# Reordering attention's SBUF pools and moving the w_down block sums into attention

## The chip, the cores and the metric

The kernel runs on one core of a Trainium2 chip. Its engines are TensorE (PE: matmuls, with PEld for its weight loads), VectorE (DVE), ScalarE (ACT), GpSimd (POOL) and SyncE (SP, which here only issues DMAs, one after the other, from one queue). The metric is the time of one execution on the device in microseconds (us).

## The reference

One layer of a bidirectional encoder over two sequences (2048 and 256 tokens of width 1024), in float32:

```python
h = rms_norm(x)
q_lat, kv_lat, z, xbc, dt = split(h @ w_in)
mla = rms_norm(softmax_attention(q_lat, kv_lat))   # 8 heads, dense over all positions
ssd = ssd_mixer(z, xbc, dt)                        # conv, forward and backward chunked scans, gate, norm
x = x + concat(mla, ssd) @ w_out
h = rms_norm(x)
y = rms_norm(x + (silu(h @ w_gate) * (h @ w_up)) @ w_down)
```

## The kernel before

Tokens are cut into 18 tiles of 128 (16 of the first sequence, 2 of the second). Every large matmul is done as three (`mm3`): both operands are split into a high part and a rest, by a copy on ACT or POOL and a subtraction on DVE (`split_w`, `split_ps`, `split`).

The stages, in order of time: (a) the input projection, whose queries, keys and values go to DRAM; (b) conv and forward scan, with the projection weights `wx0` to `wx7`, and small tables (`rows`, `offs`) loaded for each chunk by `load_rows` for `decays`; (c) attention, 8 heads of 5 query blocks (four of four tiles against 2048 keys, one of two tiles against 256); (d) `gather` (backward scan, gate, norms), `turned` (transposes) and `project` (w_out); (e) gate and up projections, in three parts of six tiles, each of 11 steps j, done as seven products of 2x2 blocks in Strassen's manner (`group`, `weights`); (f) the down projection, also of seven products, with the left operands read back from DRAM (`operand`) and the right ones (`columns`) either w_down's blocks or differences of two of them. These differences, the block sums `d_B`, are made by `sums(j)` in the last part of stage e: two loads of 512 KB into tiles `o`, four subtractions on POOL and four stores.

SBUF is handed out as stacks. The left stack after `decays` holds in stage b: `b_w0` (8 KB per partition, `wx0`), `b_st` (8), `b_w` (24), `b_w2` (32: `wx4` to `wx7`), `b_m` (12.5: `rows`, `offs`, `to`), `b_sb` (76: conv and scan tiles). In stage c the 36 KB of `mla` come first, then `c_l` (28: `pT`, `ot`), `c_q` (8), `c_kv0` (27: keys and values of even heads), `c_sb` (about 46: scores), `c_kv1` (odd heads). So the first keys lie at 72 to 99 KB, over `b_m` and the start of `b_sb`, and the first queries at 64 to 72, over `b_w2`. In stage d after `mla`: `d_st` (8: raw w_out), `d_sb` (28: `y2`, `z2`, `sc`, `ct`), `d_w` (68: split w_out, `grow`), `d_m` (24). The four tiles `o` (`op`, 4 KB each) stand on the right, from the end of stage b on, and are not used in attention. A new tile waits only for the tiles whose bytes it takes (`reuse_waits="tile"`).

The order of each queue is fixed at compile time: by a planner that walks the program with a model of time, except that inside `tc.manual_schedule(engines=...)` the named engines keep the order of the program. That holds in attention from its second block on for PE, ACT and DVE. SP's order, and the first block's, are the planner's.

Of the kernel before, what the change touches and what calls it, by code (L numbers as in the profile page):

```python
# [11 lines left out]
F32 = mybir.dt.float32  # L12
F32R = mybir.dt.float32r
I32 = mybir.dt.int32
AF = mybir.ActivationFunctionType
ALU = mybir.AluOpType
# [4 lines left out]
P = 128  # L21
D = 1024
KD = D // P
# [9 lines left out]
NF = FF // P  # L33
# [8 lines left out]
def hymba_kernel(ctx: ExitStack, tc: tile.TileContext, io, seqs, dbg=None):  # L42

    nc = tc.nc
# [26 lines left out]
    dram = ctx.enter_context(tc.tile_pool(name="dram", bufs=1, space=DRAM))  # L71
# [39 lines left out]
    def pool(stack, name, bufs, **kw):  # L111
        return stack.enter_context(tc.tile_pool(name=name, bufs=bufs, reuse_waits="tile", **kw))
# [6 lines left out]
    def split_w(hi, lo, raw, eng="pool"):  # L119
        if eng == "pool":  # L120
            nc.gpsimd.tensor_scalar(hi, raw, 1.0, 0.0, op0=ALU.mult, op1=ALU.add)
        elif eng == "act":
            nc.scalar.activation(hi, raw, AF.Copy)  # L123
        else:
            nc.vector.tensor_copy(hi, raw)
        nc.vector.tensor_tensor(lo, raw, f(hi), op=ALU.subtract)  # L126
# [248 lines left out]
    with ExitStack() as ph:  # L375
        wp0 = pool(ph, "b_w0", 1)
        st = pool(ph, "b_st", 2)
# [3 lines left out]
        with ExitStack() as inner:  # L381
            sb = pool(inner, "t_sb", 1)

            def tmp(name):
                return sb.tile([P, NT, 16], F32, name=name)
# [7 lines left out]
            u, e, s, s2, w = (tmp(f"sp{i}") for i in range(5))  # L393
# [27 lines left out]
        mp = pool(ph, "b_m", 1)  # L421
# [14 lines left out]
        for j in range(KD):  # L436
            raw = st.tile([P, KD, P], F32, name="rawx", tag="rawx")
# [56 lines left out]
        for d in range(2):  # L494
            r = mp.tile([P, SH, P], F32R, name=f"rows{d}")
            o = mp.tile([P, P], F32R, name=f"offs{d}")
            raw = sb.tile([P, SH + 1, P], F32, name="rk", tag="Y")
# [130 lines left out]
        for b in range(nb + 2):  # L628
            parts = {}
# [30 lines left out]
    op = pool(ctx, "e_o", 4, side="right")  # L660
# [5 lines left out]
        mla[t0, nt] = t  # L666


    with ExitStack() as ph:
        lp = pool(ph, "c_l", 2)  # L670
        qp = pool(ph, "c_q", 2)
        kvs = [pool(ph, "c_kv0", 1)]
        sb = pool(ph, "c_sb", 2)
        kvs.append(pool(ph, "c_kv1", 1))

# [5 lines left out]
        def step(hold=False):  # L681
            more = bool(turn)
            if turn:
                held.append(turn.popleft()())
                if not hold:
                    release()
            while len(prod) > LAG or (prod and not more):
                prod.popleft()()
                if not more:
                    break  # L690
            if late and late[0][0] <= count[0]:
                late.popleft()[1]()
            count[0] += 1
# [5 lines left out]
        def load_head(h):  # L699
            kv = kvs[h % 2]  # L700
            k = kv.tile([QKD, 2, T], F32R, name="k", tag="k")
            nc.sync.dma_start(f(k)[:NOPE], d_k[h // 2][(h % 2) * NOPE:(h % 2 + 1) * NOPE])
            nc.sync.dma_start(f(k)[NOPE:], d_kr)
            v = kv.tile([P, NT, P], F32R, name="v", tag="v")
            nc.sync.dma_start(f(v), d_v[:, h, :].rearrange("(t p) d -> p t d", p=P))
            return k, v

        def block(h, k, v, t0, nt, s0, sn):
# [93 lines left out]
            for kt in range(sn):  # L802
                turn.append(lambda kt=kt: turned(kt))
# [4 lines left out]
        def next_block():  # L808
            h, *rest = work.pop(0)
            if h not in heads:  # L810
                heads[h] = load_head(h)
            block(h, *heads[h], *rest)

        next_block()
        with tc.manual_schedule(engines={mybir.EngineType.PE, mybir.EngineType.Activation, mybir.EngineType.DVE}):
            while work:
                next_block()
            while tail:
                tail.popleft()()
            while turn or prod or late:  # L820
                step()
# [7 lines left out]
    parts = [(order[i:i + G], order[i + G:i + 2 * G]) for i in range(0, NT, 2 * G)]  # L829
# [11 lines left out]
        H[s, half] = h  # L841

    with ExitStack() as ph:
        st = pool(ph, "d_st", 2)
        sb = pool(ph, "d_sb", 2)
        wp = pool(ph, "d_w", 1)
        mp = pool(ph, "d_m", 2)
# [1 line left out]
        wo = [wp.tile([P, 2, D], F32R, name=f"wo{k}") for k in range(KD)]  # L849

        def load_wo(k):
            raw = st.tile([P, D], F32, name="rawo", tag="rawo")
            nc.sync.dma_start(raw, io["w_out"][:, k, :])
            split_w(wo[k][:, 0], wo[k][:, 1], raw, "pool" if k % 2 else "act")

# [44 lines left out]
            return y  # L900

        def turned(c, y):
            mT = mp.tile([P, 2, KD, P], F32R, name="mT", tag="mT", bufs=2)
            for part, src in enumerate((mla[c][:, 0, :], y)):
                ps = bank("t").rearrange("p (k n) -> p k n", k=4)
                for k in range(4):
                    nc.tensor.transpose(ps[:, k, :], src[:, k * P:(k + 1) * P], ident)
                split_ps(mT[:, 0, part * 4:part * 4 + 4, :], mT[:, 1, part * 4:part * 4 + 4, :], ps)
            return mT
# [39 lines left out]

    HF = NF // 2
    HK = KD // 2
    hbs.append(pool(ctx, "e_hb1", 1, side="right"))
    MS = (1, 2, 6, 5, 3, 7, 4)
    d_A = {(m, s): dram.tile([P, HF, G, P], F32, name=f"d_A{m}_{s}") for m in MS for s in range(len(parts))}
    d_B = {m: dram.tile([P, HF, 512], F32, name=f"d_B{m}") for m in (4, 5, 6, 7)}


    with ExitStack() as ph:  # L960
        rp = pool(ph, "e_raw", 3)
# [25 lines left out]

        def turned(s, half):
            columns_of(s, half, normed(parts[s][half]))

        def sums(j):

            top, low = (op.tile([P, D], F32, name="o", tag="o") for _ in range(2))
            nc.gpsimd.tensor_copy(top[:, :1], C["c11", 0][:, :1])
            nc.sync.dma_start(top, io["w_down"][j])
            nc.sync.dma_start(low, io["w_down"][j + HF])
            b11, b12, b21, b22 = top[:, :512], top[:, 512:], low[:, :512], low[:, 512:]
            for m, out, x, y in ((5, b11, b12, b11), (7, b12, b22, b12), (6, b22, b22, b11), (4, b21, b21, b22)):
                nc.gpsimd.tensor_tensor(out, x, y, op=ALU.subtract)
                nc.sync.dma_start(d_B[m][:, j], out)  # L1000

        def split(dst, src):
            nc.scalar.activation(dst[:, 0], src, AF.Copy)  # L1003
# [31 lines left out]
        def weights(s, j, m, u):  # L1035

            if m == 1:
                raw = rp.tile([P, 2, KD, P], F32, name="rawf", tag="rawf")
                nc.sync.dma_start(raw, io["w_gu"][u, :, j::HF])
                raws[u] = raw, None  # L1040
# [32 lines left out]
        X, Z, V, C = {}, {}, {}, {}  # L1073
# [59 lines left out]

        groups = [(s, j, m, u) for s in range(len(parts)) for j in range(HF) for m in MS for u in range(2)]
        AHEAD = 7
# [7 lines left out]
        for i, (s, j, m, u) in enumerate(groups):  # L1143
            group(s, j, m, u)
            if i + AHEAD < len(groups):
                weights(*groups[i + AHEAD])
            if s + 1 == len(parts) and u and m == 1:
                sums(j)
            if s + 1 < len(parts) and u:
                if m == 1 and j in (4, 7):  # L1150
                    turned(s + 1, (j - 4) // 3)
                if j == HF - 1 and m in (1, 2, 5, 3, 7, 4):
                    tokens(s + 1, m)
                    if m == 5:
                        tokens(s + 1, 6)
# [171 lines left out]
```

## Time and profile before

| what | value |
|---|---|
| median of 3 runs | 3355.14 us (3354.36 to 3357.33) |
| the profiled execution's own time | 3351.75 us |
| its span, first to last instruction | 3350.0 us |
| PE busy | 3220.2 us (96%) |
| DVE, ACT, POOL busy | 2347.6, 1703.3, 344.9 us |
| granted TensorE clock, mean | 0.984 |

The profiled execution is 3.39 us below the median. The busy time of PE says how much of a stretch holds matmuls; what is missing to the length of the stretch is time in which PE waited. The granted clock is given as a share of full speed (1.00 is 2.4 GHz, 0.50 is 1.2 GHz).

### The profile page before, as it was taken

Reading aid. Unit: us, or ns where it says so; the run is one execution under the profiler, and the core shown is the slowest. Engines: PE = TensorE matmul, PEld = TensorE weight load, DVE = VectorE, ACT = ScalarE, POOL = GpSimd, SP = SyncE. Lnnn points to the kernel's source line nnn. Section 1 sums busy time; section 2 is a strip of 40 time slices with the busy share of each in tenths; the row PEclk is TensorE's granted clock in tenths of the full one; section 3 lists DMA queues with packets and bytes.
Section 4 is the critical chain, followed back from the end, with each engine's and each line's share of the span. In section 5 each row is a group of like instructions: output and inputs, shape, how many; then the busy total and the mean of one; then the engine's idle time right before and its main releaser. Section 6 shows DMA issues by size and latency. Waiting matters only on the chain.

```text
span 3350.0 us, 48726 instructions
## 1 busy us (share of the span) xinstructions
PE 3220.2 (96%) x17834; PEld 2869.8 (86%) x17834; DVE 2347.6 (70%) x4390; ACT 1703.3 (51%) x3576; POOL 344.9 (10%) x393
## 2 busy tenths in 40 slices
PE   7999999979999999998999999999999999999998
PEld 6898999858888888887788899999999999787887
DVE  5444677758888888887774777787778776344576
ACT  5454554547777777776322455545554433332233
POOL 2121133310000000000220000000003322000000
PEclk9999999989999999999999999999999999999999
DMA  8566322141202211201553333333335446544664
GB/s 298 202 218 203 128 102 98 61 99 40 51 27 55 53 39 29 55 20 52 187 167 119 118 122 131 133 123 115 114 132 186 171 174 208 164 150 148 185 192 140
DMA packets 263823, 419.43 MB, mean 125 GB/s; under 512 B 23392, under 2 KB 175744, under 8 KB 260960
## 3 DMA queue, kind: packets, MB, share of 16 engines
q1 hardware_dynamic: 263584, 416.31, 37.5%
q8 instruction: 141, 2.31, 0.3%
q14 instruction: 98, 0.80, 0.1%
HBM read 274.57 MB, written 145.65 MB: 125 GB/s over the span
## 4 chain that ended last, share of the span: by engine, by line
PE 80%; DVE 8%; DMA 6%; ACT 2%; issue 2%; POOL 2%; SPq 0%; ACTq 0%; DVEq 0%; POOLq 0%
PE bank_ma L115 8%; PE bank_ma L117 8%; PE bank_ma L116 8%; PE bank_ma L1071 6%; PE bank_mb L1071 6%; PE bank_ta L1071 6%; PE bank_mb L115 6%; PE bank_mb L117 6%; PE bank_mb L116 6%; PE bank_ta L769 4%; PE bank_o L777 3%; PE bank_o L778 3%; PE bank_tb L769 2%; DMA rawf<-w_gu 1%; DVE ws L1004 1%
## 5 line engine op out<-in xcount | busy, mean ns | idle before, releaser
L1003 ACT ACTIVATE ws<-rawf 128x512 fp32r<-128x512 f32 x396 | 241.5, 626 | 180.7 <-DMA rawf<-w_gu 49.4
L1004 DVE TENSOR_TENSOR ws<-rawf,ws 128x512 fp32r<-128x512 f32 x396 | 278.6, 717 | 68.8 <-ACT ws L1003 67.6
L1071 PE MATMUL bank_ta<-U,ws 128*128 128x384 f32 x1584 | 301.6, 337 | 21.2 <-DVE c L1085 13.9
L1071 PE MATMUL bank_ma<-U,ws 128*128 128x384 f32 x1584 | 301.0, 336 | 4.0 <-ACT U L1003 2.1
L1071 PE MATMUL bank_mb<-U,ws 128*128 128x384 f32 x1584 | 302.6, 335 | 2.2 <-ACT c L1080 2.2
L1071 PEld LDWEIGHTS bank_ta<-U,ws 128*128 128x128 f32 x1584 | 277.5, 189 | 25.8 <-DVE c L1085 16.8
L131 DVE TENSOR_TENSOR pT<-bank_ta,pT 128x512 fp32r<-128x512 f32 (+1 forms) x352 | 239.6, 681 | 63.3 <-ACT pT L130 53.9
L1071 PEld LDWEIGHTS bank_ma<-U,ws 128*128 128x128 f32 x1584 | 277.6, 189 | 5.1 <-DVE U L1004 2.7
L1071 PEld LDWEIGHTS bank_mb<-U,ws 128*128 128x128 f32 x1584 | 276.3, 188 | 3.7 <-ACT c L1080 3.5
L130 ACT ACTIVATE pT<-bank_ta 128x512 fp32r<-128x512 f32 (+1 forms) x352 | 209.1, 595 | 117.9 <-PE bank_ta L769 117.1
L777 PE MATMUL bank_o<-pT,v 128*128 128x512 f32 x528 | 249.7, 473 | 1.9 <-ACT ot L784 1.9
L727 DVE TENSOR_REDUCE mx<-bank_ma 128x1 f32<-128x512 f32 (+1 forms) x261 | 177.0, 678 | 65.3 <-PE bank_ma L117 64.8
L769 PE MATMUL bank_ta<-ident,pr 128*128 128x128 f32 x1388 | 210.0, 273 | 2.0 <-DVE pT L131 2.0
L769 PEld LDWEIGHTS bank_ta<-ident,pr 128*128 128x128 f32 x1388 | 170.3, 140 | 48.4 <-DVE pT L131 7.3
L778 PE MATMUL bank_o<-pT,v 128*128 128x512 f32 x528 | 206.6, 391 | 0.0
L1194 ACT ACTIVATE as<-rawa 128x1408 fp32r<-128x1408 f32 x63 | 86.8, 1380 | 232.5 <-PE bank_ma L117 116.8
L475 DVE SCALAR_TENSOR_TENSOR Y<-X,cw,Y 128x256 f32<-128x256 f32 x288 | 172.4, 660 | 31.8 <-ACT X L462 30.9
L736 ACT ACTIVATE pr<-bank_ma,mx 128x512 f32<-128x512 f32 (+1 forms) x261 | 179.1, 686 | 20.5 <-DVE mx L755 19.4
L736 ACT ACTIVATE pr<-bank_mb,mx 128x512 f32<-128x512 f32 (+1 forms) x261 | 181.4, 695 | 6.9 <-DVE mx L727 4.8
L727 DVE TENSOR_REDUCE mx<-bank_mb 128x1 f32<-128x512 f32 (+1 forms) x261 | 176.9, 678 | 7.6 <-PE bank_mb L117 4.1
L117 PE MATMUL bank_ma<-hT,wx 128*128 128x256 f32 x576 | 164.7, 286 | 2.7 <-DVE wx L126 2.7
L115 PE MATMUL bank_ma<-hT,wx 128*128 128x256 f32 x576 | 166.9, 290 | 0.3 <-ACT wx L123 0.3
(415 smaller groups left out, 7970.5 us busy)
## 6 DMA issues: line engine op xcount, KB each, us to landing
rawf<-w_gu SPq DMA_DIRECT2D x66, 1024.0 KB
rawa<-d_A SPq DMA_DIRECT2D x63, 704.0 KB
d_A<-c SPq DMA_DIRECT2D x132, 192.0 KB
d_A<-s SPq DMA_DIRECT2D x99, 192.0 KB
o<-d_x SPq DMA_DIRECT2D x30, 512.0 KB
d_hT<-hT SPq DMA_DIRECT2D x7, 2048.0 KB
hT<-d_hT SPq DMA_DIRECT2D x7, 2048.0 KB
d_q<-kq SPq DMA_DIRECT2D x32, 384.0 KB
```

Source lines behind the costliest of these rows:

```text
L115: nc.tensor.matmul(ps, wh, xh, start=start, stop=False)
L116: nc.tensor.matmul(ps, wh, xl, start=False, stop=False)
L117: nc.tensor.matmul(ps, wl, xh, start=False, stop=stop)
L131: nc.vector.tensor_tensor(lo, ps, f(hi), op=ALU.subtract)
L727: nc.vector.tensor_reduce(mx[:, j:j + 1], ps[:, :m * P], axis=AX.X, op=ALU.max, negate=nch == 1)
L736: nc.scalar.activation(e[:, :m * P], ps[:, :m * P], AF.Exp, bias=bias, accum_out=rs[:, i, j:j + 1])
L769: nc.tensor.transpose(ps[:, i * P:(i + 1) * P], pr[i, kt // 4][:, kt % 4 * P:(kt % 4 + 1) * P], ident)
L777: nc.tensor.matmul(po[0][:, :n], v[:, s0 + kt, :], pT[:, 0, :n], start=kt == 0, stop=False)
L778: nc.tensor.matmul(po[0][:, :n], v[:, s0 + kt, :], pT[:, 1, :n], start=False, stop=kt == sn - 1)
L1003: nc.scalar.activation(dst[:, 0], src, AF.Copy)
L1004: nc.vector.tensor_tensor(dst[:, 1], src, f(dst)[:, 0], op=ALU.subtract)
L1071: nc.tensor.matmul(ps[:, :W], w[:, a, k, :], x[:, b, k, :], start=k + n == 0 and not more, stop=k == HK - 1 and n == 2, skip_group_check=more)
```

## The change

In attention `c_kv0` is allocated first after `mla`, then `c_q`, then `c_l`: the first keys and values lie at 36 to 63 KB, over `b_w`'s end and `b_w2`, the queries at 63 to 71 over `wx7`, and `pT` and `ot` at 71 to 99. In stage d the pool `d_st` is gone: raw w_out is loaded into the tiles `o`, `d_sb` starts right after `mla` (36 to 64, over `c_kv0`), and `mT` gets a third buffer. The block sums leave stage e; a generator `block_sums` makes them in attention, two of its steps after each block, five steps for each j. POOL is added to the engines that keep the program's order. The dummy POOL copy that tied each sum to a tile of stage e is gone.

```diff
+    def block_sums():
+        for j in range(HF):
+            top, low = (op.tile([P, D], F32, name="o", tag="o") for _ in range(2))
+            nc.sync.dma_start(top, io["w_down"][j])
+            nc.sync.dma_start(low, io["w_down"][j + HF])
+            yield
+            b11, b12, b21, b22 = top[:, :512], top[:, 512:], low[:, :512], low[:, 512:]
+            for m, out, x, y in ((5, b11, b12, b11), (7, b12, b22, b12), (6, b22, b22, b11), (4, b21, b21, b22)):
+                nc.gpsimd.tensor_tensor(out, x, y, op=ALU.subtract)
+                yield
+                nc.sync.dma_start(d_B[m][:, j], out)
     with ExitStack() as ph:
+        kvs = [pool(ph, "c_kv0", 1)]
+        qp = pool(ph, "c_q", 2)
         lp = pool(ph, "c_l", 2)
-        qp = pool(ph, "c_q", 2)
-        kvs = [pool(ph, "c_kv0", 1)]
         sb = pool(ph, "c_sb", 2)
         kvs.append(pool(ph, "c_kv1", 1))
...
-        with tc.manual_schedule(engines={mybir.EngineType.PE, mybir.EngineType.Activation, mybir.EngineType.DVE}):
+        sums = block_sums()
+        with tc.manual_schedule(engines={mybir.EngineType.PE, mybir.EngineType.Activation, mybir.EngineType.DVE, mybir.EngineType.Pool}):
             while work:
                 next_block()
+                for _ in range(2):
+                    next(sums, None)
+            for _ in sums:
+                pass
...
-        st = pool(ph, "d_st", 2)
...
-            raw = st.tile([P, D], F32, name="rawo", tag="rawo")
+            raw = op.tile([P, D], F32, name="o", tag="o")
...
-            mT = mp.tile([P, 2, KD, P], F32R, name="mT", tag="mT", bufs=2)
+            mT = mp.tile([P, 2, KD, P], F32R, name="mT", tag="mT", bufs=3)
...
-        def sums(j):
-            top, low = (op.tile([P, D], F32, name="o", tag="o") for _ in range(2))
-            nc.gpsimd.tensor_copy(top[:, :1], C["c11", 0][:, :1])
-            nc.sync.dma_start(top, io["w_down"][j])
-            nc.sync.dma_start(low, io["w_down"][j + HF])
-            b11, b12, b21, b22 = top[:, :512], top[:, 512:], low[:, :512], low[:, 512:]
-            for m, out, x, y in ((5, b11, b12, b11), (7, b12, b22, b12), (6, b22, b22, b11), (4, b21, b21, b22)):
-                nc.gpsimd.tensor_tensor(out, x, y, op=ALU.subtract)
-                nc.sync.dma_start(d_B[m][:, j], out)
...
-            if s + 1 == len(parts) and u and m == 1:
-                sums(j)
```

## Rows read from the trace of the kernel before

**Rows 1.** Busy time of each engine by stretch (us, instructions), then clock, DMA share, GB/s.

```profile
700.00:1580.00 880.00, 865.86 (x4864) 708.02 (x4864) 715.84 (x1295) 670.40 (x1663) 22.36 (x39) 0.99 0.17 41
1860.00:2500.00 640.00, 637.49 (x3698) 634.92 (x3697) 490.80 (x937) 315.27 (x603) 0.00 (x0) 1.00 0.34 125
2500.00:2840.00 340.00, 324.90 (x1856) 321.04 (x1855) 256.34 (x397) 141.28 (x267) 94.04 (x55) 1.00 0.51 179
2840.00:2880.00 40.00, 30.13 (x115) 22.96 (x114) 21.62 (x30) 16.79 (x24) 0.00 (x0) 0.87 0.85 257
```

**Rows 2.** The same view at the start and the end of attention.

```profile
640.00:690.00 50.00, 37.37 (x176) 29.23 (x174) 32.98 (x49) 18.75 (x32) 24.02 (x18) 0.84 0.20 68
690.00:702.10 12.10, 0.00 (x0) 0.03 (x1) 0.00 (x0) 1.15 (x1) 0.00 (x0) 0.50 0.96 210
702.10:730.00 27.90, 23.89 (x90) 18.00 (x91) 17.83 (x31) 15.93 (x44) 0.00 (x0) 0.83 0.66 144
1580.00:1630.00 50.00, 34.90 (x134) 26.16 (x135) 43.29 (x84) 15.26 (x33) 22.00 (x19) 0.83 0.77 267
```

**Rows 3.** SP's queue in order of time, 560 to 740 us: start, length, issue.

```profile
636.45 1.28 SPq L714 DMA_DIRECT2D q<-d_q  x2
...
651.57 1.31 SPq L511 DMA_DIRECT2D offs<-d_off  x4
664.06 0.34 SPq L608 DMA_DIRECT2D d_y<-yo  x1
...
690.30 0.52 SPq L702 DMA_DIRECT2D k<-d_k  x1
...
692.11 9.69 SPq L702 DMA_DIRECT2D k<-d_k  x1
```

**Rows 4.** Instructions on tile `wx`: duration ns min/median/max, first and last start.

```profile
L117 PE MATMUL bank_ma<-hT,wx x130: 274/283/283, 559.8 to 636.1; 128*128 128x256 f32 x130
```

**Rows 5.** The chain that ended last, around attention's start: start, length, what.

```profile
690.87 11.10 DMA k<-d_kr
...
728.79 0.23 PE bank_mb L117
```

**Rows 6.** The same chain after attention's end.

```profile
1578.64 2.53 DMA sc<-d_sb
...
1582.05 4.87 DMA ct<-d_C
...
1600.30 4.34 DMA sc<-d_sb
```

**Rows 7.** What SP's queue waited for, whole run: us in total, times, longest.

```profile
SPq L872 <- PE bank_o L778: 49.4, 1, 49.4
```

**Rows 8.** The chain in the last part of stage e, and at its end.

```profile
2577.17 5.82 DMA o<-w_down
...
2586.34 1.62 POOL o L999
...
2588.40 5.47 DMA rawf<-w_gu
...
2836.39 9.92 DMA rawa<-d_A
```

**Rows 9.** Durations by line (ns min/median/max) with POOL at work, and in attention (`pT`).

```profile
L999 POOL TENSOR_TENSOR o<-o x44: 1283/1614/3144, 2513.7 to 2830.8; 128x512 f32<-128x512 f32 x44
...
L1089 DVE TENSOR_TENSOR c<-c,c x32: 540/551/1687, 2527.9 to 2826.3; 128x384 f32<-128x384 f32 x32
...
L1085 DVE TENSOR_TENSOR c<-bank_ta,c x42: 545/550/557, 2509.9 to 2821.9; 128x384 f32<-128x384 f32 x42
...
L131 DVE TENSOR_TENSOR pT<-bank_ta,pT x338: 412/691/693, 729.7 to 1558.4; 128x512 fp32r<-128x512 f32 x167, 128x256 fp32r<-128x256 f32 x2
```

**Rows 10.** Order of time at a change of heads, SP and PE.

```profile
904.80 5.79 SPq L714 DMA_DIRECT2D q<-d_q  x2
...
911.85 0.39 PE L115 MATMUL bank_ma<-k,q 96*128 96x512 f32 x1
```

More of the change, by code (lines that the diff above doesn't have):

```diff
@@ L666, in hymba_kernel @@
         mla[t0, nt] = t
+    HF = NF // 2
+    d_B = {m: dram.tile([P, HF, 512], F32, name=f"d_B{m}") for m in (4, 5, 6, 7)}
+    def block_sums():
[9 more added lines that the diff above has]
+                nc.sync.dma_start(d_B[m][:, j], out)
     with ExitStack() as ph:
+        kvs = [pool(ph, "c_kv0", 1)]
+        qp = pool(ph, "c_q", 2)
         lp = pool(ph, "c_l", 2)
-        qp = pool(ph, "c_q", 2)
-        kvs = [pool(ph, "c_kv0", 1)]
         sb = pool(ph, "c_sb", 2)
@@ L943, in hymba_kernel @@
     mixer.close()
-    HF = NF // 2
     HK = KD // 2
@@ L956, in hymba_kernel @@
     d_A = {(m, s): dram.tile([P, HF, G, P], F32, name=f"d_A{m}_{s}") for m in MS for s in range(len(parts))}
-    d_B = {m: dram.tile([P, HF, 512], F32, name=f"d_B{m}") for m in (4, 5, 6, 7)}
     with ExitStack() as ph:
```

## Prediction

> **What bounds the kernel.** I first read the busy time by stretch [rows 1]: PE is the engine to follow. In attention it is busy 865.86 of 880 us, in the first two parts of stage e 637.49 of 640. The largest holes are at attention's start and end [rows 2], in the last part of stage e and where it hands over to stage f [rows 1]. Then, for each hole, the chain of waits and SP's queue say who ends it last: the first keys' load at attention's start [rows 3, 5], the loads of `gather` at its end [rows 6, 7], and in stage e the block sums, which stand in SP's queue ahead of the next gate and up weights [rows 8]. The change touches all four. The sum is made against the profiled execution's 3351.75 us, and 3.39 us are added at the end to come to the median.
>
> **Term 1, sums out of stage e.** Removed there: 44 subtractions and 11 copies on POOL, 22 loads, 44 stores. The chain shows what they cost [rows 8]: a load of w_down takes 5.82 us, then the subtractions run, the last store waits for the last of them, and only behind it SP issues `rawf`, which needs 5.47 us more, while DVE and then PE wait for it. POOL also slows DVE: `L1089`, with two operands in SBUF, goes from 540 to 1687 ns, while `L1085`, with one operand in PSUM, stays within 545 to 557 [rows 9]. PE idles 340 − 324.90 = 15.1 us in the last part; the earlier parts, which do the same without sums, idle 2.51 in 640 us, 1.3 in 340 [rows 1]. The gain is 15.1 − 1.3 = 13.8 us. Bounds: 10 (if some of the late `rawf` is due to its own buffers) to 15.1.
>
> **Term 2, into stage f.** In 2840 to 2880 PE idles 9.9 us, at clock 0.87 [rows 1]; the chain has `rawa`'s load of 9.92 us [rows 8], issued right after the last sum's stores and in a crowd at 257 GB/s. For comparison the 1 MB of `rawf` lands in 5.47 us [rows 8] and `rawa` is 704 KB. With the last sum's 2 MB gone, and the tiles `o` free earlier for stage f's own loads, I take the difference, 9.92 − 5.47 = 4.5, and call it 4. Bounds: 0 (other loads fill the same 10 us) to 9.9.
>
> **Term 3, attention's start.** The first keys now take the bytes of `wx3` to `wx6`, last read at 636.1 us [rows 4]. What such a tile does is in the trace: the first queries, over `b_w2`, were issued at 636.45 [rows 3]. The keys waited for `b_m` and were issued at 690.30, and landed 11.10 us after 690.87 [rows 3, 5]. So they should be there by about 650. From 690 to 702.1 PE does nothing, at a granted clock of 0.50 (1.2 GHz); from 702.1 to 730 it does 23.89 us of work at 0.83 [rows 2], which at full clock is 23.89 × 0.83 = 19.8. If the work starts at 690 and runs on, 40 − 19.8 = 20.2 us are gained. More is possible: the scores of the first block are 48 matmuls of 0.23 us [rows 5], 11 us, and from 640 to 690 PE has 12.6 idle us and DVE 17 [rows 2], so that they could run under the scan's tail; 31 is the upper end. The lower end is 1: the load's wait of 12.1 us saved, and 11.1 of it lost by the tail (first rival). I take 20. `pT` and `ot`, now over `b_m`, are needed only after the first scores, by when the scan is over; nothing for them.
>
> A row and a rule speak against this. The second head's key load could be issued only after 9.69 us of holding SP, behind the first head's 2.9 MB [rows 3]. The tail's small loads for `decays` are issued until 652.9 [rows 3], now behind the same 2.9 MB. The Trainium skill (DMA: Bandwidth & Descriptors, Queues, rings and completion order) says that each DMA engine consumes its descriptors in ring order, by which a small load waits out a large one ahead of it. By that rule alone term 3 would be 20.2 − 11.1 = 9; by the rows' slack (the last `decays` are not used for another 10 to 20 us of the tail) it stays at 20.
>
> **Term 4, attention's end.** `gather`'s tiles lay over `pT`, and its first load waited 49.4 us in SP's queue for attention's last product [rows 7]. Now they lie over the keys of even heads, dead since head 6, so these loads run under head 7. On the chain, three of them stand before the first projection: 2.53 + 4.87 + 4.34 = 11.7 us [rows 6]; I take 12. Raw w_out is in the tiles `o` before attention ends; its split copies now lie over `pT` and scores, but DVE comes to them only after the first gathers, so that costs nothing as long as DVE is the later one. Bounds: from 1580 to 1630 PE idles 15.1 us and does the other 34.90 at clock 0.83 [rows 2], so that 21 is the most; DVE is busy 43.29 of these 50 us, and if its work alone sets the start, only the first wait goes, 3. The third `mT` buffer costs and gives nothing here; PE is the later one once projection runs.
>
> **Term 5, sums into attention.** Added: 44 subtractions of 1283 ns undisturbed [rows 9], 56 us on POOL, which is busy 22.36 of 880 us there [rows 1], and 23 MB of transfers (22 × 512 KB and 44 × 256 KB) where the DMA engines are busy 17% [rows 1]. DVE's ops there read PSUM: `L131` reaches 693 ns at most [rows 9], and ops of that kind did not stretch beside POOL. Were that cover gone, 44 × 1.15 us (1687 − 540) is 50 us of DVE, in an engine with 164 idle [rows 1]. Behind a held POOL stands only `mla`'s product, one each block, whose reader is stage d. In SP's queue the stores wait for POOL, and what may stand behind them is the next queries: at a change of heads those are issued at 904.80 and used at 911.85 [rows 10], 7 us; in other blocks they have a whole block. I take 1 us as cost, bounds 0 to 20 (7 changes of heads by some 3 us).
>
> **Sum.** 13.8 + 4 + 20 + 12 − 1 = 48.8, so 3351.75 − 48.8 = 3302.95; with 3.39 that is 3306.3, or **3306 us**.
>
> **Rivals.**
> *The keys delay the scan's tail.* As above: the small loads come 11 us late, the tail ends later, and the first scores wait for it. Term 3 shrinks to some 5: 3306 + 15 = 3321. For it: the 9.69 us that SP was held [rows 3]. Against it: the tail is bound by DVE until 664 [rows 2, 3].
> *DVE sets the start of the projection.* The loads were cover for DVE's work: term 4 is 3, 3315. For it: 43.29 of 50 us busy. Against it: the chain itself names the loads.
> *The pools change nothing.* SP's queue is in order, and from 652.9 to 664 it stood still for a store [rows 3]; if the planner leaves keys and gathers behind such stores, only terms 1 and 2 are left: 3306 + 20 + 12 = 3338.
> *Slower: the sums' stores hold the queries.* A store in SP's queue waits for POOL, POOL for its place among `mla`'s products, and the next block's queries stand behind. 55 steps, two a block, reach 28 blocks; it turns the gain when each loses over 49 / 28 = 1.75 us. A load of 5.82 and a subtraction of 1.61 [rows 8] are 7.4 us; at 3 us a block it is 84, and 3390. Against it: most blocks' queries have a block's 26 us to spare (880 us [rows 1] for 32 blocks of four tiles and 8 short ones), so only changes of heads are near, and these alone (7 × 3 = 21) don't reach 49.
>
> **How the numbers follow.** Chances: forecast 0.60, keys delay the tail 0.19, DVE sets the projection 0.11, pools without effect 0.05, queries held 0.05. The forecast's own range is the ends of its terms, not all at once: 3290 to 3316. The low end of the range takes terms 3 and 4 at 31 and 20, 3306 − 19 = 3287, rounded to 3286; the high end takes in the first two rivals (3321, and both in part), 3328. A measurement here tells 0.2% (7 us) from no change. Faster: all but the last rival and a few mixed cases, 0.93. Slower 0.05, same 0.02.
>
> **What the profile after would show.** Term 1: no POOL work in stage e, and its last part as free of idle PE as the others, with `rawf` off the chain. Term 2: `rawa` landing in about 5 us. Term 3: the first keys issued near 637, no PE idle of 12 us, and score matmuls before 690. Term 4: `y`, `z`, `sc` issued before 1500 and not on the chain. Term 5: 44 POOL subtractions near 1.3 us between 700 and 1400, `L131` still at 0.69, PE as busy as before. The prediction is wrong if the scan's tail ends past 700, if PE in attention waits for `q`, or if the projection still starts 30 us after attention's last product.

## The result, and the profile after

The kernel after takes 3310.34 us (median of 4 runs, 3309.34 to 3313.65) where the kernel before, on the same chip, took 3354.75: a ratio of 0.9869 (95% interval 0.9851 to 0.9886), 44.4 us less. The forecast was 3306. The two profiled spans, 3350.0 and 3309.3 us, differ by 40.7 us, and this is where they went. The marks are starts of instructions: the scan tail's last product, the first and the last product with `v` in attention, the last addition on `xr`, the first and the last gate and up product on bank_ma, DVE's first `as`.

| stretch | before | after | less |
|---|---|---|---|
| start of the run to the scan tail's last product | 688.5 | 688.9 | −0.4 |
| from there to attention's first product | 41.4 | 26.2 | 15.2 |
| attention, first to last product | 847.8 | 848.4 | −0.6 |
| to the last `xr` addition (start and projection of stage d) | 254.9 | 252.9 | 2.0 |
| stage e, first to last gate and up product | 1006.2 | 988.8 | 17.4 |
| from there to DVE's first `as` of stage f | 6.2 | −0.9 | 7.1 |
| the rest | 505.0 | 505.0 | 0.0 |

The view of windows of the kernel after, for the stretches of [rows 1, 2] (bounds and length, then busy time and instructions of PE, weight loads, DVE, ACT and POOL, then clock, DMA share, GB/s):

```profile
640.00:690.00 50.00, 38.26 (x196) 30.18 (x194) 36.26 (x52) 20.01 (x32) 26.24 (x19) 0.90 0.48 146
690.00:702.10 12.10, 8.30 (x27) 5.98 (x27) 8.67 (x16) 5.65 (x17) 0.00 (x0) 0.86 0.79 181
702.10:715.10 13.00, 10.34 (x45) 7.82 (x45) 7.06 (x13) 10.24 (x28) 0.00 (x0) 0.87 0.48 114
715.10:1563.50 848.40, 841.53 (x4772) 689.25 (x4770) 699.33 (x1266) 655.00 (x1619) 78.29 (x83) 1.00 0.24 68
1563.50:1613.50 50.00, 32.63 (x138) 24.51 (x137) 47.68 (x109) 16.84 (x37) 20.41 (x17) 0.80 0.52 174
2805.60:2845.60 40.00, 33.49 (x138) 26.48 (x137) 21.09 (x30) 15.45 (x23) 0.00 (x0) 0.91 0.73 220
```

The hole of 12.1 us at attention's start is filled: PE does 8.30 us there, where it did nothing. But it still stands idle a quarter of the 25.1 us before the first product, and its granted clock there is 0.86 to 0.87. Attention is 0.6 us longer with 56 us more of POOL in it. The start of stage d did not improve as forecast: PE does 32.63 of 50 us there, no more than [rows 2] had, while DVE has become full, 47.68 of 50.

SP's queue of the kernel after in order of time (start, length, issue):

```profile
629.82 0.52 SPq L719 DMA_DIRECT2D k<-d_k  x1
...
636.52 5.17 SPq L731 DMA_DIRECT2D q<-d_q  x2
641.74 0.58 SPq L676 DMA_DIRECT2D o<-w_down  x1
...
648.40 5.27 SPq L511 DMA_DIRECT2D offs<-d_off  x4
...
2797.72 12.26 SPq L1196 DMA_DIRECT2D rawa<-d_A  x4
```

The first keys are issued 60 us earlier than in [rows 3]; four loads of the tail's `offs` now hold SP for 5.27 us behind them and the sums' first loads, and the scan's tail ends where it did. At the other end the first two of the four `rawa` loads are issued 7.9 us ahead of stage e's last product on bank_ma; in the kernel before it was 3.3 us, behind the sums:

```profile
2835.81 2.05 SPq L1191 DMA_DIRECT2D rawa<-d_A  x2
```

The instructions on the sums, on `pT`, and on the first maxima (duration ns min/median/max, first and last start):

```profile
L681 POOL TENSOR_TENSOR o<-o x44: 1279/1292/1582, 651.5 to 1313.2; 128x512 f32<-128x512 f32 x44
...
L131 DVE TENSOR_TENSOR pT<-bank_ta,pT x352: 412/692/693, 708.7 to 1560.8; 128x512 fp32r<-128x512 f32 x174, 128x256 fp32r<-128x256 f32 x2
...
L744 DVE TENSOR_REDUCE mx<-bank_ma x261: 416/682/693, 688.5 to 1543.0; 128x1 f32<-128x512 f32 x127, 128x1 f32<-128x256 f32 x4
```

POOL's subtractions are near their shortest time, and `L131`, which reads PSUM, is where it was [rows 9]. The first maximum starts at 688.5, 40 us after the first score: `mx` lies over a tile that the scan reads to its end.

### The profile page after: what moved, and what is told of

Its sections match the earlier page's. It is cut to its first block, busy times and chain, and to the rows that moved or that the text cites. A ratio compares the mean times of both kernels' runs of the same rounds, so it can differ in the third digit from the quotient of the medians.

```text
span 3309.3 us, 48711 instructions
## 1 busy us (share of the span) xinstructions
PE 3209.1 (97%) x17834; PEld 2864.2 (87%) x17834; DVE 2331.8 (70%) x4390; ACT 1707.2 (52%) x3576; POOL 307.1 (9%) x382
## 4 chain that ended last, share of the span: by engine, by line
PE 90%; DVE 5%; ACT 2%; DMA 2%; issue 1%; POOL 0%; SPq 0%; ACTq 0%; DVEq 0%
PE bank_mb L1078 8%; PE bank_ma L1078 8%; PE bank_ta L1078 8%; PE bank_ma L115 8%; PE bank_ma L117 8%; PE bank_ma L116 8%; PE bank_mb L115 6%; PE bank_mb L117 6%; PE bank_mb L116 6%; PE bank_ta L786 4%; PE bank_o L794 3%; PE bank_o L795 3%; PE bank_tb L786 2%; PE bank_tb L1078 2%; PE bank_o L1078 2%
## 5 line engine op out<-in xcount | busy, mean ns | idle before, releaser
L1011 DVE TENSOR_TENSOR ws<-rawf,ws 128x512 fp32r<-128x512 f32 x396 | 267.5, 687 | 96.5 <-ACT ws L1010 94.9
L131 DVE TENSOR_TENSOR pT<-bank_ta,pT 128x512 fp32r<-128x512 f32 (+1 forms) x352 | 239.6, 681 | 63.3 <-ACT pT L130 54.1
L744 DVE TENSOR_REDUCE mx<-bank_ma 128x1 f32<-128x512 f32 (+1 forms) x261 | 177.0, 678 | 50.3 <-PE bank_ma L117 49.8
```

The source lines that it names most:

```text
L131: nc.vector.tensor_tensor(lo, ps, f(hi), op=ALU.subtract)
L744: nc.vector.tensor_reduce(mx[:, j:j + 1], ps[:, :m * P], axis=AX.X, op=ALU.max, negate=nch == 1)
L1011: nc.vector.tensor_tensor(dst[:, 1], src, f(dst)[:, 0], op=ALU.subtract)
```

## The experiments

All are compared with the kernel before on the same chip. Their parts by the marks above, in us, each from one profiled execution:

| kernel | time | ratio (95% interval) | tail ends | to first product | attention | to last `xr` | stage e | to DVE's first `as` |
|---|---|---|---|---|---|---|---|---|
| before | 3354.75 | | 688.5 | 41.4 | 847.8 | 254.9 | 1006.2 | 6.2 |
| after | 3310.34 | 0.9869 (0.9851 to 0.9886) | 688.9 | 26.2 | 848.4 | 252.9 | 988.8 | −0.9 |
| 1 sums alone | 3332.78 | 0.9933 (0.9918 to 0.9947) | 689.5 | 42.6 | 847.7 | 256.3 | 989.7 | −1.0 |
| 2 keys alone | 3339.36 | 0.9958 (0.9942 to 0.9975) | 687.2 | 27.0 | 848.0 | 256.7 | 1004.2 | 6.9 |
| 3 no edits in d | 3310.32 | 0.9867 (0.9852 to 0.9882) | 689.0 | 25.5 | 848.1 | 251.1 | 989.2 | −1.0 |
| 4 maxima early | 3311.79 | 0.9873 (0.9858 to 0.9888) | 691.1 | 22.2 | 848.8 | 254.3 | 989.9 | −1.0 |
| 5 less DVE | 3297.67 | 0.9842 (0.9826 to 0.9859) | 688.9 | 26.0 | 848.4 | 242.7 | 988.2 | −1.0 |
| 6 no subtraction | 3334.83 | 0.9954 (0.9939 to 0.9968) | 691.0 | 41.5 | 847.9 | 255.9 | 990.3 | 5.2 |
| 7 POOL alone | 3317.67 | 0.9901 (0.9884 to 0.9917) | 687.9 | 25.5 | 848.2 | 252.9 | 995.2 | 0.5 |
| 8 weights' pool first | 3316.37 | 0.9902 (0.9882 to 0.9921) | 687.6 | 25.5 | 848.3 | 259.7 | 990.5 | −1.0 |
| 9 stores by POOL | 3339.49 | 0.9962 (0.9947 to 0.9977) | 689.2 | 41.4 | 847.7 | 256.2 | 996.5 | 4.6 |
| 10 gain in weights | 3313.77 | 0.9884 (0.9869 to 0.9898) | 692.1 | 26.0 | 848.1 | 253.2 | 990.4 | −1.0 |
| 11 and ACT alone | 3309.14 | 0.9868 (0.9852 to 0.9885) | 688.5 | 26.2 | 848.5 | 251.7 | 990.6 | −1.0 |
| 12 and same places | 3303.30 | 0.9856 (0.984 to 0.9873) | 687.8 | 25.5 | 848.1 | 247.0 | 988.0 | −1.0 |

How far a column can be trusted is read from kernels that don't differ in it: the tail's end lies anywhere from 687.6 to 692.1 in the kernel after and in runs 5, 7, 8, 10, 11 and 12, which are the same until then; stage e from 988.0 to 990.6 in those without sums there, and at 1006.2 and 1004.2 in the two that have them as before. The column of the last `xr` lies from 254.9 to 256.3 in the kernel before and runs 1, 6 and 9, and from 252.9 to 254.3 in the kernel after and runs 4 and 7. What follows the last column is not in the table: from DVE's first `as` to the end it is 502.3 to 506.7 us in all fourteen, 504.7 before and 504.6 after.

### 1 and 2: each half alone

Run 1 has the sums in attention, with the pools and stage d as before. Run 2 has the reordered pools of attention and nothing else:

```diff
+        kvs = [pool(ph, "c_kv0", 1)]
+        qp = pool(ph, "c_q", 2)
         lp = pool(ph, "c_l", 2)
-        qp = pool(ph, "c_q", 2)
-        kvs = [pool(ph, "c_kv0", 1)]
```

> Only the block sums are moved into attention; pools and raw w_out stand as before. The marks of the two traces (last scan product, last attention product, last projection sum, last gate/up product, end) give the parts of the 40.7 us: attention's start 14.8, attention itself -0.6, attention's end to stage e 2.0, stage e 17.4, into stage f 7.2. Theory A, the parts add and are independent: this kernel keeps -0.6, 17.4 and 7.2, so 24 us faster than before, about 3331, with attention starting as before. Theory B, the keys and the sums help or hinder each other (the sums' first loads stand among the scan's small loads at attention's start): the gain differs from 24 by more than 4 us.

> Only attention's pools are reordered, so that the first keys lie over the projection weights; sums and stage d stand as before. Theory A, the parts add: about 15 us faster than before, 3340, nearly all of it by the first attention product (715 instead of 730 us), and stage e as slow as before in its last part (15 us of idle PE). Theory B, without the sums' loads of 2 MB among the scan's small loads the first scores come earlier: 18 to 22 us faster.

The sums alone took 0.0067 off the ratio, the pools alone 0.0042; together 0.0109, and with the whole change 0.0131, within what the intervals allow. In time that is 19.8 and 13.2 us, 33.0 of the 44.4; whether the missing 11 are spread or something that only both halves together give is not settled. By the columns each half does its own: run 1 has the whole gain of stage e and of the way into f and none at attention's start, run 2 the reverse. Run 1 came 4.2 us short of its 24, just past the 4 that divide its theories: it gains 23.7 in stage e and into f and loses 5.5 in parts that it does not change. Neither gains anything in stage d. Putting the sums into attention cost the stretch from first to last product nothing (847.7 against 847.8).

### 3: without the edits of stage d

The kernel after with raw w_out in its own pool and two `mT` buffers, as before:

```diff
+        st = pool(ph, "d_st", 2)
...
-            raw = op.tile([P, D], F32, name="o", tag="o")
+            raw = st.tile([P, D], F32, name="rawo", tag="rawo")
...
-            mT = mp.tile([P, 2, KD, P], F32R, name="mT", tag="mT", bufs=3)
+            mT = mp.tile([P, 2, KD, P], F32R, name="mT", tag="mT", bufs=2)
```

> The changed kernel with stage d as before: raw w_out in a pool of its own in front of the gathers' tiles, two mT. Theory A, VectorE's own work sets the start of the projection, so that early loads are worth only 2 us by the end of stage d: 3312, within 3 us of the changed kernel. Theory B, the early loads are worth the three waits that stood on the chain before, 12 us: 3320 or more.

The time is that of the kernel after. The early raw weights and the third `mT` are worth nothing here. They do change the order of work: the first `xr` addition comes 49.4 us behind attention's last product in run 3, 38.3 in the kernel after and 54.5 in the kernel before, but from it to the last `xr` it takes 201.7, 214.6 and 200.4 us. So an early first addition does not mean an early end.

### 4: maxima that need not wait for the scan

The kernel after with the tiles `mx` and `rs` in a small pool of their own, placed in SBUF that is free earlier:

```diff
+        mxp = pool(ph, "c_mx", 4)
...
-                mx = sb.tile([P, 5], F32, name="mx", tag="mx", bufs=4)
+                mx = mxp.tile([P, 5], F32, name="mx", tag="mx")
```

> The changed kernel with the score maxima (mx) and row sums (rs) in a pool of their own, over the projection weights, where before they lay over the conv outputs Y that the last scan still reads. In the changed kernel seven scores were done by 691 us, but no maximum before 688.5. Theory A, that overlap held the maxima back, and with them the banks: maxima run from about 655 us, the first attention product comes at 708 to 712 us instead of 715, 3 to 7 us faster than the changed kernel, 3303 to 3307. Theory B, the ramp after 690 us is set by ScalarE's exponentials, which wait for the scan's banks anyway: no more than 1 us.

The first product stands 22.2 us behind the tail's end, where all other kernels with early keys have 25.5 to 27.0; so the late maxima do cost some 3 to 5 us from that mark. But the tail ended at 691.1, the first product came at 713.3 (theory A had 708 to 712), and the time did not fall. DVE's and ACT's order of time in run 4 shows what came next on the way (start, length, what, and the idle time before it):

```profile
684.56 0.16 DVE L773 TENSOR_REDUCE mx<-mx 128x1 f32<-128x4 f32 x1
...
691.57 0.60 ACT L599 ACTIVATE ns<-bank_tb 128x512 f32<-128x512 f32 x1 [5.85 <-PE bank_tb L593]
692.07 0.68 ACT L754 ACTIVATE pr<-bank_ma,mx 128x512 f32<-128x512 f32 x1
```

The first tile's maximum was complete at 684.6, and still ACT's first exponential ran at 692.07, right behind `ns`, the scan tail's last operation on ACT. Whether the early maxima delayed the tail, or its end lay late within its own spread of 687.6 to 692.1, is not settled by this run.

### 5: less work for DVE at stage d's start

The kernel after with the low part of w_out copied by ACT:

```diff
-            split_w(wo[k][:, 0], wo[k][:, 1], raw, "pool" if k % 2 else "act")
+            if k % 2:
+                nc.gpsimd.tensor_scalar(wo[k][:, 0], raw, 1.0, 0.0, op0=ALU.mult, op1=ALU.add)
+            else:
+                nc.scalar.activation(wo[k][:, 0], raw, AF.Copy)
+            nc.scalar.activation(wo[k][:, 1], raw, AF.Copy)
```

> The kernel after, with the rest of each block of w_out copied by ACT in place of the subtraction on DVE (leaves out that subtraction, so the low part of each output weight is the block itself). Theory A, DVE sets the start of the projection: eight operations that stood at 1.2 to 2.3 us each leave DVE's queue there, so the stretch from attention's last product to the last xr add, 252.9 us in the kernel after, gets 8 to 12 us shorter and the time is about 3300 us. Theory B, the weights or TensorE's clock set it: at most 2 us shorter, 3308 to 3311 us.

The stretch fell from 252.9 to 242.7 us, the time to 3297.67: theory A. The edit also frees the tiles `o` for the next load of w_out without waiting for DVE; what that gives is not told apart from DVE's time. The chain of the kernel after at that place says the same (start, length, what):

```profile
1569.02 0.98 DVE rs_u L145
...
1572.94 2.21 DVE wo L126
...
1578.37 4.47 DMA o<-w_out
1582.85 1.61 DVE mla L919
1584.46 1.45 DVE y L920
```

One load of w_out is left on it; nearly all else is DVE. The windows from 10 us after attention's last product show what the eight subtractions held up, first in the kernel after (three slices):

```profile
1573.50:1583.50 10.00, 2.61 (x7) 1.38 (x5) 9.88 (x16) 2.39 (x5) 3.97 (x4) 0.50 0.94 349
1583.50:1593.50 10.00, 7.23 (x26) 5.18 (x26) 10.00 (x15) 3.36 (x7) 4.81 (x4) 0.73 0.38 138
1593.50:1603.50 10.00, 10.00 (x51) 8.45 (x51) 10.00 (x30) 1.79 (x5) 2.50 (x3) 1.00 0.27 79
```

and then in run 5 (two):

```profile
1573.30:1583.30 10.00, 8.02 (x25) 5.89 (x24) 9.42 (x27) 5.36 (x11) 3.36 (x4) 0.54 1.02 364
1583.30:1593.30 10.00, 10.00 (x51) 8.37 (x50) 9.83 (x22) 5.88 (x10) 4.72 (x4) 1.00 0.36 118
```

DVE is as full in both, with 27 and 22 instructions in place of 16 and 15, so it comes to the gathers sooner; PE has 8.02 and 10.00 in place of 2.61 and 7.23, and the granted clock is at 1.00 ten us earlier.

### 6, 7 and 9: what the sums cost stage e

Three runs take the sums apart. Run 6 is the kernel before without the subtractions:

```diff
-                nc.gpsimd.tensor_tensor(out, x, y, op=ALU.subtract)
                 nc.sync.dma_start(d_B[m][:, j], out)
```

> The kernel before, with the sums' loads, their tying copies and their stores kept in stage e and the 44 subtractions on POOL left out (so the stored blocks are w_down's own and the output is wrong by that). Stage e took 1006.2 us before and 988.8 us after. Theory A, the sums' transfers and stores in SP's queue hold back the loads of the next weights: at least 10 of these 17.4 us stay, the time is 3345 to 3357 us. Theory B, POOL's subtractions slow DVE while they run: at least 10 of them go, the time is 3335 to 3343 us.

Run 7 is the kernel after with the subtractions and the tying copies in stage e, on two tiles loaded once:

```diff
+            if s + 1 == len(parts) and u and m == 1:
+                pool_alone(j)
```

> The kernel after, with 44 subtractions on POOL and the eleven tying copies added in the last part of stage e, at the places of before, on two tiles that are loaded once (no other load, no store; their results are not used). Theory A, the transfers were what the sums cost there: stage e takes at most 3 us more than 988.8, the time is 3308 to 3314 us. Theory B, POOL's subtractions were: 10 us or more are added, 3320 to 3330 us.

Run 9 is the kernel before with the stores issued by POOL, so that SP's queue need not stand for them:

```diff
-                nc.sync.dma_start(d_B[m][:, j], out)
+                nc.gpsimd.dma_start(d_B[m][:, j], out)
```

> The kernel before, with the 44 stores of the sums issued by POOL, which makes the sums, in place of SP. Without POOL's subtractions stage e was 990.3 us against 1006.2 before (15.9 less), and the same subtractions without transfers cost 6.4 us there. Theory A, SP's queue stands at stores that wait for POOL, and the loads of the next weights behind them: some 9 us of stage e go, 996 to 999 us, and the time is 3343 to 3347 us. Theory B, POOL's slowing of DVE is all of it, more so where the loads spread it out: at most 3 us go, 3350 to 3355 us.

Run 6: all the transfers and none of the subtractions give 990.3 us, within the spread of the kernels without sums, so the transfers themselves cost at most some 2 us. That refutes run 6's theory A as it was put; its theory B, that at least 10 of the 17.4 us go, holds. But run 7 fits neither of its own: POOL's work alone adds 6.4 us, more than the 3 of theory A and less than the 10 of theory B. Run 9, made to tell whether the two act together, took 9.7 us off stage e (7.7 against run 2, whose sums are those of before), as its theory A had it with 996 to 999; the time, 3339.49, is below the 3343 to 3347 that went with it. The windows of the last part of stage e, its first 100 us and its rest, in the kernel before:

```profile
2500.30:2600.30 100.00, 94.43 (x538) 92.90 (x538) 85.70 (x121) 46.18 (x82) 25.82 (x15) 1.00 0.47 168
2600.30:2839.10 238.80, 229.28 (x1312) 226.95 (x1311) 170.34 (x277) 94.80 (x184) 68.22 (x40) 1.00 0.53 184
```

in the kernel after:

```profile
2484.10:2584.10 100.00, 99.23 (x569) 98.16 (x568) 84.72 (x136) 47.92 (x86) 0.00 (x0) 1.00 0.32 113
2584.10:2805.60 221.50, 221.50 (x1280) 221.50 (x1279) 152.12 (x261) 96.59 (x181) 0.00 (x0) 1.00 0.34 120
```

in run 7, with POOL's work and no transfers:

```profile
2482.20:2582.20 100.00, 94.59 (x540) 93.06 (x539) 88.35 (x120) 44.81 (x81) 27.68 (x15) 1.00 0.29 105
2582.20:2810.10 227.90, 227.15 (x1310) 226.83 (x1310) 186.37 (x276) 96.23 (x185) 67.87 (x40) 1.00 0.35 124
```

and in run 9, with everything but the stores in SP's queue:

```profile
2502.20:2602.20 100.00, 94.65 (x533) 93.44 (x532) 86.64 (x121) 46.40 (x82) 29.56 (x27) 0.98 0.47 168
2602.20:2831.30 229.10, 229.10 (x1324) 229.10 (x1323) 176.59 (x278) 98.56 (x186) 77.95 (x72) 1.00 0.56 194
```

The two costs lie in different places. In the first 100 us DVE has 85 us to do, and with POOL beside it PE is idle for 5.4 of these whether there are transfers or not (runs 7 and 9), without POOL for 0.8. After that DVE has room, with POOL alone PE is idle for under 1 us, and what PE lost before, 9.5 of 238.80, is gone when the stores leave SP's queue. The waits of the same stretch name the wait, in the kernel before (engine, tile and line, releaser: us in total, times, longest):

```profile
DVE S L1049 <- DMA rawf<-w_gu: 69.1, 10, 9.3
...
ACT ws L1003 <- DMA rawf<-w_gu: 35.6, 10, 5.1
PE bank_ta L1071 <- DVE c L1085: 10.0, 8, 2.2
```

and in run 9:

```profile
DVE S L1049 <- DMA rawf<-w_gu: 37.2, 10, 6.4
...
ACT ws L1003 <- DMA rawf<-w_gu: 4.2, 5, 1.6
PE bank_ta L1071 <- DVE U L1004: 2.5, 1, 2.5
```

DVE's and ACT's waits for `rawf` fall from 104.7 to 41.4 us, and PE's 10.0 us behind DVE's `c` are gone. So of the 17.4 us, 9.7 are SP's queue behind stores that wait for POOL, 6.4 POOL beside DVE, and what is left, 1.3, is no more than the spread of some 2 us that each of these numbers has.

On the way into stage f the order is another: run 6 keeps 5.2 of the 6.2 us and run 9 4.6, run 7 has 0.5. There it is the transfers that cost, not the subtractions.

### 8, 10, 11 and 12: a version with less for DVE

Run 8 puts the pool of the split weights ahead of the gathers' tiles:

```diff
-        sb = pool(ph, "d_sb", 2)
         wp = pool(ph, "d_w", 1)
+        sb = pool(ph, "d_sb", 2)
```

> The kernel after, with the pool of the split output weights put ahead of the gathers' tiles, so that the first three weights lie in SBUF that attention's even heads leave free and their splits can run under the last head. Theory A, DVE sets the projection's start: some three subtractions of 1.2 us come out of the start of stage d, 3 to 5 us less from attention's last product to the last xr add, 3305 to 3308 us. Theory B: no difference, 3309 to 3311 us.

The first `xr` addition came 35.1 us after attention's last product, 38.3 in the kernel after, which alone would be theory A; yet the whole stretch is 6.8 us longer and the time 3316.37, which neither theory had. From the first `xr` addition to the last it takes 224.6 us, not 214.6.

Runs 10 and 11 take 36 operations from DVE: the gain, laid out as a column for each block of rows, goes into the rows of w_out, the normalisations to ACT. In run 11 ACT also makes all eight rounded copies:

```diff
-            split_w(wo[k][:, 0], wo[k][:, 1], raw, "pool" if k % 2 else "act")
+            g = gmix[:, k:k + 1]
+            nc.scalar.activation(wo[k][:, 0], raw, AF.Copy, scale=g)
+            nc.vector.scalar_tensor_tensor(wo[k][:, 1], raw, g, f(wo[k][:, 0]), op0=ALU.mult, op1=ALU.subtract)
...
-            nc.vector.scalar_tensor_tensor(mla[c][:, 0, :], mla[c][:, 0, :], r[:, 0:1], grow[:, :SW], op0=ALU.mult, op1=ALU.mult)
-            nc.vector.scalar_tensor_tensor(y, y, r[:, 1:2], grow[:, SW:], op0=ALU.mult, op1=ALU.mult)
+            nc.scalar.activation(mla[c][:, 0, :], mla[c][:, 0, :], AF.Copy, scale=r[:, 0:1])
+            nc.scalar.activation(y, y, AF.Copy, scale=r[:, 1:2])
```

> The kernel after, with the gain of the two norms multiplied into the rows of w_out while they are split (the same count of instructions) and the two normalisations of each tile moved from DVE to ACT: 36 operations of 0.75 to 1.6 us leave DVE, and the broadcast gain row is not loaded. Theory A, DVE bounds the start of stage d: about five tiles' share of them, 7 to 10 us, leave that start, and the stretch from attention's last product to the last xr add goes from 252.9 to about 245 us, the time to 3300 to 3304 us. Theory B, only the subtractions of the weights count there, the gathers being ahead of their use: at most 2 us, 3308 to 3311 us.

> The kernel of the run before this one (gain in the weights), with all eight rounded copies of w_out made by ACT, so that POOL's four no longer run beside DVE. Theory A, POOL's copies stretch DVE's operations at that start (a two-column operation took 0.97 us there in place of 0.15): 2 to 4 us less than the run before, 3297 to 3301 us. Theory B, POOL's other operations of the gathers do that, or ACT becomes late: within 1.5 us of the run before, or slower.

Run 10 gained nothing (253.2 us for the stretch, and 3313.77 is above both theories); run 11 is 4.6 us faster than run 10 by the time, but by the profiles only 1.5 lies in this stretch, and 3.6 is the earlier end of the scan's tail, where the two are the same kernel. What POOL's copies cost is not shown by it. Run 11's first `xr` addition, though, came at 33.6 us, 4.7 earlier than in the kernel after; as in run 8, the rest of the projection gave it back. In these three runs the projection's products read longer. Run 11 (ns min/median/max):

```profile
L116 PE MATMUL bank_ma<-wo,mT x144: 392/396/628, 1580.5 to 1808.6; 128*128 128x512 f32 x144
```

In the kernel after and the others it is 387/389 or 390. What the three share is that tiles of stage d lie elsewhere. By the order and sizes of the pools, run 8 moves `wo` and the gathers' tiles and leaves `mT` where it was; in runs 10 and 11 a tile of 32 bytes a partition stands in place of one of 4 KB, behind `wo` and ahead of the pool of `mT` and `xr`, which moves. Run 12 gives it the old size and changes nothing else:

```diff
-        gmix = wp.tile([P, KD], F32, name="gmix")
+        gmix = wp.tile([P, D], F32, name="grow")[:, :KD]
```

> The kernel of the run before this one (gain in the weights, rounded copies by ACT), with the gain's tile made as large as the broadcast row was, so that every tile of stage d lies where it lies in the kernel after. Where tiles of stage d had moved (two runs here and the one with the weights' pool first) the projection's matmuls read 394 to 396 ns at the median, in all other runs 389 to 390. Theory A, where operands lie in SBUF sets that: the median returns to 389 ns, the 4 to 6 us that 864 matmuls lose by 5 to 7 ns come back, the start of stage d keeps its gain of 4 to 5 us over the kernel after, and the time is 3302 to 3306 us. Theory B, it comes from what ACT and DVE do beside them: the median stays at 395 ns and the time at 3307 to 3311 us.

Theory A. The median is 389 again, and it is not the chip: run 9 ran on that of runs 10 and 11, runs 5 to 7 on that of run 8, and all read 389.

```profile
L116 PE MATMUL bank_ma<-wo,mT x144: 387/389/628, 1578.7 to 1802.3; 128*128 128x512 f32 x144
```

The stretch takes 247.0 us and the kernel 3303.30 (3302.42 to 3307.61), no run of which reaches into those of the kernel after (3309.34 to 3313.65). So it beats both kernels, the kernel after by 5.9 us when each is set against the kernel before that ran beside it (50.3 and 44.4 us less), though the two intervals of the ratios overlap.

## Why the prediction was right, and where not

**The time** was right, 3306 against 3310.34, in part by luck, because errors of both signs met. Against the profile the sum of terms was 48.8 us where 40.7 came: terms 1 and 2 were 6.7 us too small, terms 3 and 4 14.8 too large, term 5 0.4 too pessimistic, and the scan's tail ended 0.4 later. Of the 8.1 us between, 3.7 came back by chance: the profiled execution lies 3.0 us below the median before and 0.75 above it after, so that the medians differ by 44.4.

**Term 1, 13.8, measured 17.4**, above its upper bound of 15.1. The mechanism stands: the last store waits for POOL and SP issues `rawf` only behind it; run 9 took out this step alone and got 9.7 us, and run 7 showed POOL's slowing of DVE as the second share, 6.4. The size was read from PE's idle time, 15.1 us [rows 1]. It did vanish, to 0.8 (321.50 − 320.73). But the busy time of the same work fell too, from 323.70 to 320.73, and the two make 14.3 + 3.0 = 17.3. The holes hide partly in the busy time: the 12 matmuls of this part that start behind one are recorded with 440 to 446 ns where 334 is the median, and the last one ahead of a hole counts with all its 334 ns, while starts otherwise stand 173 apart. After the change 3 start behind a hole.

**Term 2, 4, measured 7.1**, within its bounds. That `rawa` would land faster was the smaller part of it: 4.6 us are its earlier issue (7.9 against 3.3 us ahead of the stage's last product), in a queue that no longer holds the sums' loads and stores, and 2.5 the way from issue to ACT's first `as` (5.6 against 8.1). The page of the kernel after still has loads on the chain there:

```profile
2815.66 5.22 DMA rawd<-w_down
...
2822.28 4.20 DMA rawd<-w_down
...
2829.17 3.22 DMA rawd<-d_B
```

**Term 3, 20, measured 15.2** from the tail's end. The keys came as worked out, issued at 629.82 and there at 640.2. The step that was too large is "if the work starts at 690 and runs on": it does not run on. Only 6 of the 16 first score tiles were complete before 690, and behind the tail the chain of maximum, exponential and free bank paces PE. The late maxima are not all of it: in run 4, where they were early, it was 6 too; the seventh waited for the bank of the scan tail's last `ns`, and the eighth for the first exponential, which ACT ran behind that `ns`. The waits from 685 to 716 us in the kernel after:

```profile
ACT pr L753 <- DVE mx L772: 7.1, 3, 3.5
...
PE bank_mb L115 <- ACT pr L753: 3.3, 3, 1.8
```

**The rival of late small loads** did not come: four loads of `offs` held SP for 5.27 us, and the tail ended at 688.9, within its spread. The order that the Trainium skill (DMA: Bandwidth & Descriptors, Queues, rings and completion order) states for the descriptors of a ring is not what that row shows: SP stood between the four issues, for the queries' loads and the sums' to land, and the same row is 4.37 us long in run 1, where the keys come late. The sum by that rule, 9, was not what came.

**Term 4, 12, measured 2.0.** This is the step that failed, and the rival that DVE sets the projection's start, priced at 3, is what happened. Against it the prediction said that "the chain itself names the loads" [rows 6]. They were the last to end; with the loads early, from 1514 us on, DVE's work stood behind them, 47.68 of 50 us. The first `xr` addition did come 16.2 us sooner (38.3 against 54.5 us behind attention's last product), but from there the projection took 14.2 longer (214.6 against 200.4), and PE did no more work in the first 50 us (32.63, and 34.26 in the kernel before from the same mark). Its first full slice is that of 1593.50, 30.0 us behind the last product; by this measure a sign of being wrong that the prediction had named came. Run 3 shows that the change's edits in stage d gave nothing, run 5 that eight long operations off DVE give 10.2 us there, run 12 that 36 others, with POOL's four copies gone from beside DVE, give 5.9.

**Term 5, −1, measured −0.6**, and in run 1, with the sums and the old pools, 0.1 the other way: the sums cost attention nothing that these runs can tell. SP's queue did stand for POOL in attention, 290.0 us in 40 waits, and no queries came late:

```profile
SPq L683 <- POOL o L681: 290.0, 40, 16.9
```

So the rival that the sums' stores hold the queries, the one slower outcome, had its wait and not its price: between 716 and 1560 us PE waited 6.2 us in all, for ACT and DVE alone and never for a load. That the pools change nothing is refuted by run 2: its reordered pools alone bring the first product 14.4 us nearer to the tail's end.

## What to carry to other kernels

A wait that ends last names what to remove, not what removing it gives: look at how full the next engine is in the same window, here DVE with 43.29 of 50 us, and price the stage by that engine's work. A store that waits for a slow engine costs most where loads stand behind it in one queue; moving the work to where the queue has nothing urgent took out 17.4 us, and another queue for the stores would have brought 9.7 of them. When pools are moved or shrunk, compare the durations of untouched instructions that use tiles behind them, since run 11 and run 12 differ in nothing but a tile's size.

## What the runs showed of the hardware

**Small DVE operations wait out POOL's.** At stage d's start `L145` works on two columns and two tiles in SBUF. Its shortest is 143 ns, and three of 18 took 969 to 1006. Each of these began while a POOL operation ran and ended within 0.02 us of that operation's end; in the whole run none of the 194 that no POOL operation overlaps took more than 165 ns. `L909`, one of whose operands is in PSUM, took 692 ns the one time that it ran beside POOL's work, where its shortest is 676. In the kernel after:

```profile
L145 DVE TENSOR_TENSOR rs_u<-rs_u,rs_ms x18: 143/156/1006, 1569.0 to 1613.0; 128x2 f32<-128x2 f32 x15, 128x1 f32<-128x1 f32 x3
...
L909 DVE TENSOR_TENSOR to<-bank_o,dfs x6: 676/678/692, 1565.6 to 1610.2; 128x512 f32<-128x512 f32 x6
```

Two stretched operations of DVE, each followed by the one of POOL that ran beside it (start, length):

```profile
1585.84 0.99 DVE L145 TENSOR_TENSOR rs_u<-rs_u,rs_ms 128x2 f32<-128x2 f32 x1
...
1585.34 1.48 POOL L121 TENSOR_SCALAR wo<-o 128x1024 fp32r<-128x1024 f32 x1
...
1581.82 1.11 DVE L141 TENSOR_SCALAR rs_ms<-ss 128x2 f32<-128x2 f32 x1
...
1581.64 1.27 POOL L910 TENSOR_TENSOR y<-y,to 128x512 f32<-128x512 f32 x1 [5.59 <-DVE rs_y L146]
```

The stretch is thus not in proportion to the operation: a tiny one can cost as much as what is left of POOL's instruction, here 1.0 us. The Trainium skill (SBUF — State Buffer, Who interferes with whom) states that a DVE instruction with two inputs in SBUF contends with one of GpSimd that reads SBUF; the rows of `L145` agree. `L141` reads one tile only and was stretched as well, from 146 to 1115 ns. In the prediction this effect was counted for large operations alone [rows 9].

**A matmul's time depends on where its tiles lie.** 864 products of the projection read 394 to 396 ns at the median in runs 8, 10 and 11 and 389 or 390 in all others. It is not the clock: from 1640 to 1800 us the granted clock is 1.00 and PE busy throughout in runs 11 and 12 alike, and the first did 751 matmuls there, the second 763. Between runs 11 and 12 the stretch from the first to the last `xr` addition differs by 218.1 − 213.5 = 4.6 us, 864 × 6 ns being 5.2. Since run 8 moves `wo` and runs 10 and 11 `mT`, the place of one operand alone does not decide; what in their places does was not tried.
